# A statically ordered decoder layer: coarser places for background steps, a longer scan price, and pages waited for

## The chip, the cores and the metric

One Trainium2 chip, one of its cores. The metric is device microseconds of one execution of the program. Times of instructions come from one execution that the hardware profiler recorded; its microseconds are counted from the first recorded instruction.

## The reference

One decoder layer on x (1024 tokens, 1024 features), float32. `proj = rmsnorm(x) @ w_in` is cut into attention q, k, v (8 heads of 64), and q, k, v, output gate and input and forget gates of an mLSTM (4 heads of 128). The attention sums three dilated windows. The mLSTM goes by chunks: with `b` the running sum of the log forget gate and `m` a running maximum, it builds the scaled states and the heads' outputs. Both halves are normed and go through `w_out`; the result is added to x. Then follows a gated feed-forward part (`w_ffn_up` to 2 x 2816, a causal convolution of 3 taps, silu(gate) * value, `w_ffn_down`), added again, and a last norm.

## The kernel before, in words

**How precise matmuls are made.** A float32 product is made of three matmuls of a faster 4-byte type: every operand is split into a high and a low page, and `mm3` (the helper after `copy`) issues high x high, high x low, low x high. So matmuls come in threes.

**Stages.** The projections come first (`project`): 19 units, written out by hand in the string `order`. A unit "m" (mLSTM q or k of one head) or "h" (attention q and k of one head) makes two banks of 512 tokens, each from 8 threes of 512 columns, k = 0 to 7. A unit "g", "v" or "a" (gates, mLSTM values, attention values) makes 8 blocks of 128 tokens, each from 8 threes of 256 or 260 columns. The weights of unit n are named w*n* in the trace (w3 is the unit v0, w16 to w18 are the last three attention heads). Then `output` makes the product with `w_out`: first the mLSTM half (weights w0, w1 on the tiles ymh, yml), then, when all four attention groups are there, the attention half (w2, w3 on yh, yl). Its blocks are made by `o_block`, 4 threes of 512 columns each. Last come `upward` (tiles xb, W) and `downward` (A, B), which the change does not touch.

**What sets the order.** Every engine runs its instructions in the order in which the program was written, and waits in that order. The order is made when the program is built. The work is held in lanes: Python generators with a priority (a lower number goes first). A lane yields `need(...)`: the tiles it needs, free pages (`pg`, of 48 in SBUF, with `keep` more left over), free PSUM banks (`bk`). `Lanes.run` looks at the model's time on PE ("now"), computes for each lane the time at which its need is met (`when`), and takes the first lane by priority whose need has been met for 0.6 us (`SLACK`); if there is none, the one that is met first. The model (`Clock`) adds a price to an engine's time for each instruction; `Clock.cost` holds the prices. A `project` or `output` lane (priorities 10 and 11) always has something to run and so is what PE does when no other lane is ready: the **foreground**. All other lanes are **background**. A background step can come between two foreground matmuls only where the foreground yields.

Before the change an "m" or "h" unit yields after every three matmuls, a "g", "v" or "a" unit after every second three (`if k % 2`), and `o_block` after every three.

**The gate lane** (`gates`, priority 4). When the gates are projected, 16 transposes bring them into rows, DVE makes two scans over 1024 elements (`tensor_tensor_scan`: tiles gb and gm), then uu and four writes into the tile `rows`. PE transposes `rows` in 8 pieces of 68 x 68 and multiplies it 8 times with `sel` (8 columns each). The mLSTM lanes wait for what comes out. `Clock.cost` has no case for a scan: it falls to the last line for DVE, 0.095 + n * 0.0011 us.

**The attention lanes.** `stacks` (one per head, priority 3) takes the two projected banks, multiplies them by R into the page t, and splits t into the pages q1, q2 and kS with five copies and two subtractions on ACT and DVE. `scores` goes through heads and pairs of query blocks (matmuls bank<-kS,q), `soft` takes the exponent on ACT, `trans` transposes (bank<-ident,P), `evac_T` splits the result (tile PT), `values` multiplies (bank<-PT,av), `fold` and `att_norm` end a group of two heads, `att_t` and `y_trans` transpose it into yh, yl. At most three heads may lie ready in `heads` (`HL`) before `project` holds back the next. `stacks` takes its first page after `yield need(pg=4, keep=2, ...)` and the pages q1, q2, kS right after the second bank is evacuated, with no look at when those pages become free.

The output's attention half needs all of `yT["a", g]` and both its weights; the last of these (w3) is split only when `output` has taken w2.

Of the kernel before, what the change touches and what calls it, by code (L numbers as in the profile page):

```python
# [29 lines left out]
class Clock:  # L30
# [84 lines left out]
    def cost(self, eng, op, outs, ins, k):  # L115
        n = 1
        for d in (ins if op == "tensor_reduce" else outs)[0].shape[1:]:
            n *= d
        from_psum = any(a.tensor.name in self.psum for a in ins)
        if eng == "pe":  # L120
            dt = ins[0].dtype
            if dt == F32R:
                return n / 2246 + 0.004
            if dt == BF:
                return max(n, 64) / 2400 + 0.003
            return 0.11 if op == "transpose" else 2 * max(2 * n, 256) / 2300
        if eng == "act":
            c = (0.05 if from_psum else 0.1) + n * 0.000833 + 0.09 * (len(ins) + len(outs) - 2)
            for v in list(k.get("_a", ())) + list(k.values()):
                if isinstance(v, AF) and v in self.SETS:  # L130
                    if self.table not in (None, self.SETS[v]):
                        c += 1.3
                    self.table = self.SETS[v]
            return c
        if eng == "dve":
            if op == "reciprocal":
                return n * 0.0063
            fast = op in ("tensor_copy", "tensor_scalar", "memset") and not from_psum
            return 0.095 + n * (0.00058 if fast else 0.0011) + (0.06 if from_psum else 0) + (0.05 if len(ins) > 2 else 0) + 0.01 * (len(outs) - 1)
        if OP.pow in k.values():  # L140
            return 0.3 + n * 0.165
        return 0.1 + n * 0.00228
# [76 lines left out]
def need(*tiles, pg=0, bk=0, cond=None, keep=0, kb=0):  # L219

    return tiles, pg, bk, cond, keep, kb
# [3 lines left out]
def tile_hybrid_layer(ctx, tc, xT, x, w_t, w_v, w_g, w_o, w_uq, w_dq, params, fnw, c_id, c_att, c_sel,  # L225
# [23 lines left out]
    def page(name, dt=F32):  # L249
        slot[0] = freep.pop(0)  # L250
        t = pages.tile([128, PGW], dt, tag="pg", name=name)
        clk.floor[t.tensor.name] = slot[0]
        return t

    def free(*ts):
        for t in ts:
            freep.append(clk.last(t))
# [5 lines left out]
    def bank(name=None):  # L263
        t = min(freeb, key=clk.last)
        freeb.remove(t)
        return t
# [49 lines left out]
    def mm3(o, lh, ll, rh, rl, start, stop):  # L316
        pe.matmul(o, lh, rh, start=start, stop=False)
        pe.matmul(o, lh, rl, start=False, stop=False)
        pe.matmul(o, ll, rh, start=False, stop=stop)
# [64 lines left out]
    def wneed(whl, **k):  # L384
        return need(*[t for p in whl for t in p], **k)
# [8 lines left out]
    for o in order.split():  # L394
        n = int(o[1])
# [171 lines left out]
    def fin_ready(ps, hf):  # L567

        if hf < len(ps) and "R" in flags:
            return max(clk.ready(ps[hf]), 1e-9)  # L570
        return False

    def ml_conv(c, ps):

        h, isk = divmod(c, 2)
        for hf in range(2):
            yield need(pg=0 if hf else 2, cond=lambda: fin_ready(ps, hf))
            if hf == 0:
                z = page("mz")
                a = page("mqk")  # L580
            dve.tensor_mul(z[:, H[hf]], ps[hf], R[:, H[hf]])
            freebank(ps[hf])
        ch = 4 * isk + h
        cw = lambda j: pr[:, P_CW + ch * 4 + j:P_CW + ch * 4 + j + 1]
        yield need(z)
        act.activation(a[:, :S], z[:, :S], AF.Identity, scale=cw(3), bias=pr[:, P_CB + ch:P_CB + ch + 1])
        for j in (2, 1, 0):
            sh = 3 - j
            yield need(a)
            dve.scalar_tensor_tensor(a[:, sh:S], z[:, :S - sh], cw(j), a[:, sh:S], op0=OP.mult, op1=OP.add)  # L590
        free(z)
        yield need(a)
        act.activation(a[:, :S], a[:, :S], AF.Silu)
        qk[c] = a
# [42 lines left out]
    def project():  # L637

        for n, (kind, arg) in enumerate(plan):
            if n == len(plan) - 2:  # L640
                flags.add("late")
            if n == len(plan) - 1:
                flags.add("last")
            npg = {"mv": 2, "av": 4, "g": 4 if arg == 0 else 0}.get(kind, 0)
            yield need(pg=npg, cond=lambda: n in feed.done and (kind != "att" or len(heads) < HL))
            whl = feed.get(n)
            if kind in ("ml", "att"):
                (wh, wl), = whl
                ps = []
                for hf in range(2):  # L650
                    yield wneed(whl, bk=1, kb=FGB - 1 if "R" in flags else 1)
                    p = bank("fg")
                    if hf == 0:
                        lanes.add(ml_conv(arg, ps) if kind == "ml" else stacks(arg, ps), 3)
                    for k in range(8):
                        ks = slice(k * 128, (k + 1) * 128)
                        mm3(p, wh[:, ks], wl[:, ks], xh[k][:, H[hf]], xl[k][:, H[hf]], k == 0, k == 7)
                        if hf and n == len(plan) - 1:
                            free(xh[k], xl[k])
                        yield need()  # L660
                    ps.append(p)
            else:
                w = 260 if kind == "g" else 256
                if kind == "g" and arg == 0:
                    sg.extend(page(f"sg{i}") for i in range(4))
                if kind == "mv":
                    for h in (2 * arg, 2 * arg + 1):
                        t = page(f"va{h}")
                        vap.append(t)
                        va.append(t[:, :1032].rearrange("p (c j) -> p c j", j=129))  # L670
                        pool.memset(va[h][:, :, 128:129], 1.0)
                if kind == "av":
                    av[arg] = [page(f"av{arg}{i}", F32R) for i in range(4)]
                for i in range(8):
                    yield wneed(whl, bk=1, kb=FGB - 1)
                    p = bank("fg")
                    ts = slice(i * 128, (i + 1) * 128)
                    for k in range(8):
                        wh, wl = whl[k // 4]
                        ks = slice((k % 4) * w, (k % 4 + 1) * w)  # L680
                        mm3(p[:, :w], xh[k][:, ts], xl[k][:, ts], wh[:, ks], wl[:, ks], k == 0, k == 7)
                        if k % 2:
                            yield need()
                    lanes.add(evac_n(kind, arg, i, p, w), 3)
            feed.put(whl)
        flags.add("projected")

    def evac_n(kind, arg, i, p, w):
        yield need(p)
        {"g": evac_g, "mv": evac_mv, "av": evac_av}[kind](arg, i, p[:, :w])  # L690
        freebank(p)
        if i == 7:
            flags.add((kind, arg))
# [208 lines left out]
    def stacks(h, ps):  # L902
        for hf in range(2):
            yield need(pg=0 if hf else 4, keep=2, cond=lambda: fin_ready(ps, hf))
            if hf == 0:
                t = page("t")
            dve.tensor_mul(t[:, H[hf]], ps[hf], R[:, H[hf]])
            freebank(ps[hf])
        if h == 7:
            free(R)  # L910
        q1 = page("q1", F32R)
        q2 = page("q2", F32R)
        kS = page("kS", F32R)
        lo, up = slice(0, 64), slice(64, 128)
        A = slice(0, S)
        yield need(t)
        copy(q1[lo, A], t[lo, A])
        copy(kS[up, A], t[up, A])
        yield need(q1)
        dve.tensor_sub(q2[lo, A], t[lo, A], f32(q1[lo, A]))  # L920
        copy(q2[up, A], t[lo, A])
        yield need(kS)
        dve.tensor_sub(kS[lo, A], t[up, A], f32(kS[up, A]))
        yield need(q2)
        copy(q1[up, A], f32(q2[lo, A]))
        free(t)
        den = small.tile([128, 8], F32, name="aden", bufs=4)
        heads[h] = (q1, q2, kS, den)
# [184 lines left out]
    def o_block(p, hf, i, key, whl):  # L1113
        sl = slice(hf * 512, (hf + 1) * 512)
        ts = slice(i * 128, (i + 1) * 128)
        for k in range(4):
            yh, yl = yT[key, k]
            wh, wl = whl[k // 2]
            ws = slice((k % 2) * 512, (k % 2 + 1) * 512)
            mm3(p, yh[:, ts], yl[:, ts], wh[:, ws], wl[:, ws], k == 0, k == 3)  # L1120
            yield need()

    def add_h(i, hf, p):
        yield need(p, hp[i])
# [570 lines left out]
```

## Time and profile before

| | us |
|---|---|
| median of 3 runs | 1223.29 |
| lowest, highest | 1223.19, 1224.44 |
| the profiled execution's own time | 1226.69 |
| its span, first to last instruction | 1224.9 |

A row of the timeline gives the start, the time that the instruction (or a run of like ones) took, the engine, and what it wrote from what. Matmuls are pipelined, so the time that one took (0.39 us for 512 columns) is longer than its share of PE: what a matmul costs is the time from its start to the next one's start. PEld is the load of the stationary operand, which overlaps. "Idle before" in square brackets names what an engine waited for. The granted clock is a share of full speed: 1.00 is 2.4 GHz, 0.50 is 1.2 GHz, and a number in between is a mean over the stretch.

### The profile page before, as it was taken

What the parts mean: (1) busy time and instruction counts of PE and PEld (TensorE: products, weight loads), DVE (VectorE), ACT (ScalarE), POOL (GpSimd) and SP (SyncE); (2) the same over time, 40 slices, a digit from 0 to 9 for tenths busy, and PEclk for the clock granted to TensorE, in tenths of its full rate; (3) what the DMA queues carried; (4) which work ended last, traced back from release to release, by engine and by line L of the source; (5) the groups of instructions that cost most, each with busy time, mean ns of one, the idle gap of its engine ahead of it and who ended that gap; (6) DMA issues with size and microseconds to landing.
All of it is one profiled execution on the core that took longest, in us unless ns stands there. A gap on an engine that the chain in (4) does not pass through costs nothing.

```text
span 1224.9 us, 17354 instructions
## 1 busy us (share of the span) xinstructions
PE 1214.1 (99%) x6366; PEld 1028.9 (84%) x6366; DVE 889.7 (73%) x1642; ACT 589.5 (48%) x1139; POOL 255.3 (21%) x176
## 2 busy tenths in 40 slices
PE   9999999999999999999999999999999999999997
PEld 7899898988998888888888888888888888888886
DVE  6634573658886988645998787768777788988965
ACT  5464253437764675445763533434344353343553
POOL 0421032120212210211043413333332310000001
PEclk9999999999999999999999999999999999999999
DMA  9360917564256679243566663775633379423333
GB/s 364 151 225 18 206 70 275 114 162 165 94 125 167 225 254 245 69 146 142 121 221 179 207 232 113 205 242 132 194 115 126 127 299 410 135 86 97 94 102 139
DMA packets 64077, 208.01 MB, mean 170 GB/s; under 512 B 6644, under 2 KB 9972, under 8 KB 59000
## 3 DMA queue, kind: packets, MB, share of 16 engines
q1 hardware_dynamic: 57048, 135.80, 31.3%
q0 software_dynamic: 4352, 34.60, 14.0%
q10 hardware_dynamic: 2592, 36.50, 8.8%
q8 instruction: 50, 0.82, 0.3%
q14 instruction: 35, 0.29, 0.1%
HBM read 182.76 MB, written 93.32 MB: 225 GB/s over the span
## 4 chain that ended last, share of the span: by engine, by line
PE 96%; DVE 2%; DMA 1%; issue 0%; ACT 0%; POOLq 0%; POOL 0%; ACTq 0%; DVEq 0%
PE bank L153 96%; DMA h<-in_x_dram 1%; DVE P L153 0%; DMA w0r<-in_w_t_dram 0%; DVE rows L153 0%; DVE gb L153 0%; DVE gm L153 0%; DVE ams L153 0%; DVE uu L153 0%; DVE nmx L153 0%; ACT lf L153 0%; ACT sq L153 0%; DVE hq L153 0%; DVE h L153 0%; DVE OT L153 0%
## 5 line engine op out<-in xcount | busy, mean ns | idle before, releaser
L153 PE MATMUL bank<-xb,W 128*128 128x512 f32 x1848 | 428.9, 394 | 0.0
L153 PEld LDWEIGHTS bank<-xb,W 128*128 128x128 f32 x1848 | 346.9, 188 | 80.8
L153 PE MATMUL bank<-B,A 128*128 128x512 f32 x924 | 213.9, 393 | 0.0
L153 PEld LDWEIGHTS bank<-B,A 128*128 128x128 f32 x924 | 173.6, 188 | 40.1
L153 POOL TENSOR_TENSOR W<-ur,W 128x512 fp32r<-128x512 f32 x94 | 123.7, 1331 | 277.4 <-ACT W L153 134.5
L153 DVE SCALAR_TENSOR_TENSOR ua<-bank,pr,ua 128x512 f32<-128x512 f32 (+3 forms) x208 | 133.8, 646 | 25.1 <-ACT ua L153 19.0
L153 ACT ACTIVATE ua<-bank,pr 128x512 f32<-128x512 f32 (+1 forms) x84 | 64.9, 774 | 146.3 <-DVE bank L153 146.3
L153 DVE TENSOR_TENSOR bank<-bank,ut 128x512 f32<-128x512 f32 x84 | 58.2, 697 | 33.1 <-PE bank L153 31.7
L153 ACT ACTIVATE W<-ur 128x512 fp32r<-128x512 f32 x122 | 71.5, 622 | 16.1 <-DMA ur<-in_w_uq_dram 10.2
L153 ACT ACTIVATE A<-g 128x512 fp32r<-128x512 f32 x75 | 46.4, 626 | 60.0 <-DVE g L153 48.4
L153 POOL TENSOR_TENSOR rs<-st,half 128x1 f32<-128x1 f32 x16 | 11.2, 698 | 265.2 <-DVE st L153 265.2
L153 ACT ACTIVATE P<-P,nmx 128x128 f32<-128x128 f32 (+3 forms) x64 | 49.4, 773 | 25.0 <-DVE nmx L153 24.6
L153 DVE CUSTOM_DVE_ANT_0 P<-bank,matt 128x512 f32<-128x512 f32 (+3 forms) x96 | 50.6, 552 | 13.7 <-PE bank L153 13.5
L153 DVE TENSOR_TENSOR ut<-ut,bank 128x512 f32<-128x512 f32 x66 | 45.0, 682 | 19.7 <-PE bank L153 19.1
L153 DVE TENSOR_TENSOR A<-g,A 128x512 fp32r<-128x512 f32 x75 | 50.9, 685 | 7.0 <-ACT A L153 6.7
L153 DVE TENSOR_TENSOR hq<-hq,bank 128x512 f32<-128x512 f32 x56 | 36.6, 680 | 24.7 <-PE bank L153 24.7
L153 DVE TENSOR_TENSOR PT<-bank,PT 128x512 fp32r<-128x512 f32 (+1 forms) x80 | 47.8, 629 | 9.1 <-ACT PT L153 8.8
L153 ACT ACTIVATE B<-br 128x512 fp32r<-128x512 f32 x70 | 43.2, 621 | 22.7 <-PE bank L153 9.7
L153 DVE TENSOR_TENSOR B<-br,B 128x512 fp32r<-128x512 f32 x76 | 51.5, 683 | 3.3 <-ACT B L153 3.1
L153 DVE TENSOR_TENSOR W<-ur,W 128x512 fp32r<-128x512 f32 x60 | 43.9, 738 | 7.1 <-ACT W L153 6.5
L153 ACT ACTIVATE PT<-bank 128x512 fp32r<-128x512 f32 (+1 forms) x71 | 37.1, 551 | 23.6 <-PE bank L153 20.9
L153 PE MATMUL bank<-PT,av 128*128 128x256 f32 (+1 forms) x320 | 46.6, 279 | 0.0
(352 smaller groups left out, 2435.3 us busy)
## 6 DMA issues: line engine op xcount, KB each, us to landing
usum<-in_w_uq_dram POOLq DMA_DIRECT2D x4, 5632.0 KB, 34.1
ur<-usum SPq DMA_DIRECT2D x88, 256.0 KB, 4.1
ur<-in_w_uq_dram SPq DMA_DIRECT2D x66, 256.0 KB, 4.5
usum<-in_w_uq_dram ACTq DMA_DIRECT2D x2, 5632.0 KB, 20.7
usum<-usum ACTq DMA_DIRECT2D x2, 5632.0 KB, 21.8
tsum<-in_w_dq_dram POOLq DMA_DIRECT2D x4, 2816.0 KB, 19.0
gp<-ua SPq DMA_DIRECT2D x22, 512.0 KB, 3.0
g<-gp SPq DMA_DIRECT2D x22, 512.0 KB, 7.7
```

What stands on the lines that cost most here:

```text
L153: r = f(*a, **k)
```

## The change

A scan gets a price of its own in the model. "m" and "h" units yield after every second three matmuls, "g", "v" and "a" units after every fourth, `o_block` after every second. In `stacks` the lane yields once for t and three pages together, ahead of taking them. No instruction of the program is added or removed by the text of the diff; what changes is the order in which the lanes write them, and the pages and banks that they get.

```diff
--- before.py
+++ after.py
@@ -135,6 +135,8 @@
         if eng == "dve":
             if op == "reciprocal":
                 return n * 0.0063
+            if op == "tensor_tensor_scan":
+                return 0.05 + n * 0.0022
             fast = op in ("tensor_copy", "tensor_scalar", "memset") and not from_psum
             return 0.095 + n * (0.00058 if fast else 0.0011) + (0.06 if from_psum else 0) + (0.05 if len(ins) > 2 else 0) + 0.01 * (len(outs) - 1)
         if OP.pow in k.values():
@@ -657,7 +659,8 @@
                         mm3(p, wh[:, ks], wl[:, ks], xh[k][:, H[hf]], xl[k][:, H[hf]], k == 0, k == 7)
                         if hf and n == len(plan) - 1:
                             free(xh[k], xl[k])
-                        yield need()
+                        if k % 2:
+                            yield need()
                     ps.append(p)
             else:
                 w = 260 if kind == "g" else 256
@@ -679,7 +682,7 @@
                         wh, wl = whl[k // 4]
                         ks = slice((k % 4) * w, (k % 4 + 1) * w)
                         mm3(p[:, :w], xh[k][:, ts], xl[k][:, ts], wh[:, ks], wl[:, ks], k == 0, k == 7)
-                        if k % 2:
+                        if k % 4 == 3:
                             yield need()
                     lanes.add(evac_n(kind, arg, i, p, w), 3)
             feed.put(whl)
@@ -908,12 +911,12 @@
             freebank(ps[hf])
         if h == 7:
             free(R)
+        yield need(t, pg=3)
         q1 = page("q1", F32R)
         q2 = page("q2", F32R)
         kS = page("kS", F32R)
         lo, up = slice(0, 64), slice(64, 128)
         A = slice(0, S)
-        yield need(t)
         copy(q1[lo, A], t[lo, A])
         copy(kS[up, A], t[up, A])
         yield need(q1)
@@ -1118,7 +1121,8 @@
             wh, wl = whl[k // 2]
             ws = slice((k % 2) * 512, (k % 2 + 1) * 512)
             mm3(p, yh[:, ts], yl[:, ts], wh[:, ws], wl[:, ws], k == 0, k == 3)
-            yield need()
+            if k % 2:
+                yield need()
 
     def add_h(i, hf, p):
         yield need(p, hp[i])
```

## Rows read from the trace of the kernel before

**Rows 1.** The page: busy time, share of the span and instructions of each engine.

```profile
PE 1214.1 (99%) x6366; PEld 1028.9 (84%) x6366; DVE 889.7 (73%) x1642; ACT 589.5 (48%) x1139; POOL 255.3 (21%) x176
```

**Rows 2.** Engines by stretch: start:end, length, busy us (instructions) per engine, clock, DMA share, GB/s.

```profile
114.50:124.10 9.60, 8.61 (x48) 8.20 (x47) 3.53 (x7) 2.84 (x9) 3.62 (x2) 0.64 0.18 26
...
267.00:525.00 258.00, 256.66 (x1592) 227.81 (x1591) 203.20 (x488) 159.42 (x306) 54.08 (x26) 1.00 0.55 160
...
575.50:1004.60 429.10, 429.10 (x1859) 347.97 (x1858) 338.32 (x521) 190.25 (x336) 132.38 (x102) 1.00 0.57 178
```

**Rows 3.** Who made PE wait, whole span: us in total, times, longest.

```profile
PE bank L153 <- DVE lnk L153: 1.2, 1, 1.2
PE bank L153 <- DVE rows L153: 1.0, 2, 0.7
PE bank L153 <- DVE h L153: 0.8, 1, 0.8
PE bank L153 <- DVE w0h L153: 0.7, 1, 0.7
PE bank L153 <- ACT P L153: 0.4, 1, 0.4
```

**Rows 4.** DVE in order of time, 104 to 130: start us, us, instruction, count, idle before.

```profile
107.21 2.28 DVE L153 TENSOR_TENSOR_SCAN gb<-rst,lf 4x1024 f32<-4x1024 f32 x1 [3.56 <-ACT lf L153]
109.42 2.25 DVE L153 TENSOR_TENSOR_SCAN gm<-lf,li 4x1024 f32<-4x1024 f32 x1
111.78 1.21 DVE L153 TENSOR_TENSOR uu<-gb,gm 4x1024 f32<-4x1024 f32 x1
...
115.00 1.07 DVE L153 TENSOR_TENSOR rows<-uu,gm 4x896 f32<-4x896 f32 x1
116.00 1.21 DVE L153 TENSOR_TENSOR urow<-uu,urow 4x1024 fp32r<-4x1024 f32 x1
```

**Rows 5.** PE in order of time, 108 to 130.

```profile
114.49 0.28 PE L153 MATMUL bank<-w3l,xh 128*128 128x256 f32 x1
114.61 0.28 PE L153 MATMUL bank<-w3h,xl 128*128 128x256 f32 x1
115.22 0.25 PE L153 MATMUL bank<-ident,rows 68*128 68x68 f32 x1 [0.33 <-DVE rows L153]
116.12 0.66 PE L153 MATMUL bank<-ident,rows 68*128 68x68 f32 x7 [0.66 <-DVE rows L153]
116.71 1.46 PE L153 MATMUL bank<-rows,sel 4*128 4x8 f32 x8
118.11 0.58 PE L153 MATMUL bank<-w3h,xh 128*128 128x256 f32 x1
...
124.03 0.28 PE L153 MATMUL bank<-w3h,xh 128*128 128x256 f32 x1
124.15 0.28 PE L153 MATMUL bank<-w3l,xh 128*128 128x256 f32 x1
```

**Rows 6.** PE in order of time, 423 to 447, transposes between the matmuls of a projection.

```profile
427.15 0.49 PE L153 MATMUL bank<-ident,P 128*128 128x128 f32 x3
...
427.71 0.40 PE L153 MATMUL bank<-xl,w18h 128*128 128x512 f32 x1
...
428.87 0.93 PE L153 MATMUL bank<-ident,P 128*128 128x128 f32 x7
...
429.87 0.39 PE L153 MATMUL bank<-xl,w18h 128*128 128x512 f32 x1
...
434.26 0.39 PE L153 MATMUL bank<-xh,w18h 128*128 128x512 f32 x1
...
434.95 0.64 PE L153 MATMUL bank<-PT,av 128*128 128x256 f32 x4
```

**Rows 7.** PE in order of time, 490 to 512.

```profile
496.25 0.48 PE L153 MATMUL bank<-w0h,ymh 128*128 128x512 f32 x1
...
497.02 1.04 PE L153 MATMUL bank<-PT,av 128*128 128x256 f32 x8
```

**Rows 8.** PE in order of time, 510 to 530.

```profile
524.90 0.40 PE L153 MATMUL bank<-w2h,yh 128*128 128x512 f32 x1
```

**Rows 9.** POOL in order of time, 497 to 520.

```profile
519.87 2.41 POOL L153 TENSOR_TENSOR w3l<-wr,w3h 128x1024 fp32r<-128x1024 f32 x1 [8.53 <-ACT w3h L153]
```

**Rows 10.** DMA issues: out<-in, engine, count, KB each, median us from issue to landing.

```profile
wr<-in_w_t_dram SPq DMA_DIRECT2D x13, 512.0 KB, 8.8
```

**Rows 11.** ACT in order of time, 404 to 424, and PE, 423 to 447.

```profile
419.05 1.06 ACT L153 ACTIVATE q<-q 64x1024 fp32r<-64x1024 f32 x1
...
422.97 0.97 PE L153 MATMUL bank<-kS,q 128*128 128x128 f32 x6
```

## The prediction

> **What bounds the kernel now.** The page's busy shares come first: PE is busy 99% of the span, DVE 73%, ACT 48% [rows 1]. A busy PE need not be a fast one, so the windows by stage come next. From 575.5 to 1004.6 us PE starts 1859 matmuls, nearly all of 512 columns, in 429.10 us, 231 ns each: nothing is left between them. From 267 to 525 (attention) PE is idle 258.00 - 256.66 = 1.34 us. One stretch stands out: from 114.5 to 124.1 PE starts 48 matmuls in 9.6 us at a mean granted clock of 0.64 [rows 2]. The list of waits says the same: PE waited 4.1 us in all, 1.9 of it at the start (lnk, w0h), 1.0 for `rows`, 1.2 in attention (h, P) [rows 3]. So PE's own work sets the time. A new order that takes no matmul away can only return these waits and the clock that they cost, or add new ones.
>
> **The scan's price.** The model charged 0.095 + 1024 x 0.0011 = 1.22 us for a scan. The two scans and the next DVE step start at 107.21, 109.42 and 111.78, so one takes 2.2 to 2.4 [rows 4]. The new price is 0.05 + 1024 x 0.0022 = 2.30. So all that follows the scans is planned 2 x 1.08 = 2.16 us later. What was wrong is seen on PE: the last w3 matmul before the transposes starts at 114.61, and 0.12 later PE is free, but the first transpose starts at 115.22 and the second at 116.12 [rows 5], when DVE's write of `rows` at 115.00 + 1.07 = 116.07 is over [rows 4]. Seven transposes take 116.71 - 116.12 = 0.59, 0.08 each, so PE lost 115.22 - 114.73 = 0.49 and 0.90 - 0.08 = 0.82, in all **1.31 us**. A lane is taken at the first yield 0.6 us after its planned readiness, and yields there came every 6 x 0.12 = 0.72: the plan had `rows` ready between 113.4 and 114.1, where the chip had it at 116.07. With 2.16 more and yields every 1.44, PE comes to the transposes between 116.2 and 118.3: behind 116.07, so the wait goes. PE runs w3 matmuls meanwhile, of which enough are left: 27 from 118.11 to 124.03 alone [rows 5]. The mLSTM lanes behind `rows` start about 2 us later, under the next unit's matmuls.
>
> The clock is the larger part. After the waits and the narrow matmuls (8 of 68 columns, 8 of 8 columns), 27 w3 matmuls take 124.03 - 118.11 = 5.92 us, 0.22 each, where the same ones take 0.12 before and after [rows 5]: PE ran at 1.2 GHz instead of 2.4. That costs 5.92 - 27 x 0.12 = **2.7 us**, and the eight 8-column matmuls, 1.40 us together, may hold another 0 to 0.7 (at a narrow transpose's 0.08 each they would take 0.7). Without the waits the light stretch is 0.6 + 1.4 = 2.0 us instead of 118.11 - 114.73 = 3.4. No row shows whether the clock falls after that. The ends are "falls as before" (0 gained) and "stays" (2.7 to 3.4 gained). Nearest is attention, where PE waits of 0.8 and 0.4 us [rows 3] lie among narrow matmuls and the clock stays at 1.00 [rows 2]. I take "stays".
>
> The Trainium skill, "TensorE: Matmul & The Clock Gate", Part 4, says that PE transposes do not count as PE being busy for the clock. By that rule the stretch would still look idle and the time would be rival 1's; attention's 1.00, with its many transposes, speaks against it only weakly, because wide matmuls stand among them.
>
> **Yields after every six.** First, does a change from foreground to background cost PE anything? Three transposes and the matmul behind them take 427.71 - 427.15 = 0.56, seven and the matmul 429.87 - 428.87 = 1.00 [rows 6]. Four more transposes cost 0.44, 0.11 each; 0.56 - 3 x 0.11 = 0.23 is left for the matmul, and three plain ones take 434.95 - 434.26 = 0.69, 0.23 each [rows 6]. A switch costs nothing, so fewer switches gain **0**.
>
> What coarser yields cost is delay. A background step that is ready waits until a six ends, at most one more three, 0.69 us. From 423 to 500 the foreground runs in 22 stretches between background steps; 14 hold an odd number of threes (one at 434.26 [rows 6], the last but one at 496.25 [rows 7]) and would end 0.69 later: up to 14 x 0.69 = 9.7 us if all lie on one chain, 0 if other background work fills in. What hides it is foreground: the attention half starts at 524.90 [rows 8] and its last input, w3l, is ready at 519.87 + 2.41 = 522.28 [rows 9]. The **cover is 2.6 us**; beyond it PE waits. I take 0, because DVE, 203 of 258 us busy there [rows 2], paces the heads as much as PE's places do, and because what background loses foreground gains: the last heads' projections end earlier. Both ends, 0 and 9.7 - 2.6 = 7.1, are kept. The 1.2 us of waits in attention may go or come back elsewhere: I take 0 and keep -1.2.
>
> Work that is moved with the lanes: weight loads on SP (512 KB, 8.8 us to land) [rows 10] and their splits on POOL (2.41 us each) [rows 9] go out up to 0.69 us later, against a unit of 48 x 0.23 = 11 us that they run ahead. Nothing else on SP, ACT's or POOL's queues changes in number.
>
> **Pages in `stacks`.** The lane now waits for t and three pages before it takes them. Behind it wait five copies and two subtractions on ACT and DVE, then `scores`. Where cover is small, the last write of q ends at 419.05 + 1.06 = 420.11 and the head's scores start at 422.97 [rows 11]: 2.9 us. Pages that come later than that would add to attention's delay above, earlier ones change nothing: 0, with the same 2.6 us behind it. A gain is bounded by attention's 1.2 us of PE waits, which are counted already.
>
> **The sum.** Against the profiled execution's own 1226.69 us (span 1224.9 and 1.8 around it): 1226.69 - 1.31 - 2.7 = 1222.7. The median of the runs is 1223.29, 3.40 lower. I cannot see whether the timed runs have the fall of the clock. The gap is about its price (2.7 to 3.4), which would fit runs that mostly lack it; then only 1.31 is to be had. I count half of 2.7: 1223.29 - 1.31 - 1.35 = **1220.6**.
>
> **Rivals.** (1) **The clock falls anyway**, after 2.0 us of narrow matmuls. For it: the fall came in just this stretch. Against: 1.31 us of plain idling is gone. Time 1223.29 - 1.31 = 1222.0. Chance 0.18.
>
> (2) **Attention ends too late**: slower. Place: between the last head's scores and 524.90. For it: 14 of 22 stretches get longer, and the cover is 2.6. Against: DVE's share, earlier projections. At a delay d PE waits d - 2.6: at 9.7 the time is 1220.6 + 7.1 = 1227.7; it is slower than before by over 0.2% (2.45 us, about what a measurement here tells from no change) from d = 2.6 + 2.7 + 2.45 = 7.7 on, or from 5.0 if that wait lowers the clock too, at 2.7. Chance 0.27.
>
> (3) **The change does not do what it says**: the order is made anew as a whole, another step before `rows` (the chain has four more DVE writes) is planned too early, and PE waits as before: 1223.3, give or take attention's 1.2. Chance 0.08.
>
> **How the numbers follow.** The forecast has 0.47; its own range is 1223.29 - 1.31 - 3.4 = 1218.6 to 1222.0. It is faster by over 0.2% if at least 2.45 - 1.31 = 1.14 of the clock's 2.7 us is in the timed runs, or part of it and attention's 1.2: four in five of 0.47, 0.38; with rival 2 below d = 2.8 (0.05) and rival 3's luck (0.01), faster 0.44. Same: 0.09 of the forecast, 0.18, 0.05 of rival 3, and 0.06 of rival 2, 0.38. Slower: 0.16 of rival 2 and 0.02 of rival 3, 0.18. The range goes from 1223.29 - 1.31 - 3.4 - 1.2 = 1217.4 to rival 2's 1227.7; beyond it lies attention's delay with a fall of the clock on top.
>
> **What would show it.** Right: the row of PE's waits for `rows` is gone, the transposes of `rows` start after DVE's last write, the granted clock is 1.00 from 114 to 125, the w3 matmuls keep 0.12, and the stretches of foreground between background steps are all multiples of six without a wait of PE before w2h,yh. Rival 1: no wait but a clock under 1.00 there. Rival 2: a wait of PE, or w3l within a few tenths of the first w2h,yh. Wrong altogether: gains or losses behind 575, where I expect PE at 231 ns a matmul as now.

## The result and the profile after

The changed kernel takes 1230.38 us (median of 4 runs, 1230.10 to 1230.62); the kernel before took 1223.72 beside it. The ratio is 1.0053, 95% interval 1.0041 to 1.0065: **slower by half a per cent**, 6.7 us, where 1220.6 was forecast and the range ended at 1227.7. The profiled execution's own time is 1230.62, its span 1228.8 us. All medians here and below are of executions in the chip's fast state; one of the six of kernel e9 below (1319.21 us at a granted clock of 0.85) is left out.

The page's busy shares, as [rows 1]:

```profile
PE 1214.0 (99%) x6366; PEld 1027.6 (84%) x6366; DVE 893.0 (73%) x1649; ACT 583.1 (47%) x1131; POOL 251.2 (20%) x175
```

PE is as busy as before, and the other shares move by at most one point: a page of shares does not show the loss. The windows by stretch do, as [rows 2] (start:end, length, busy us and instructions of PE, PEld, DVE, ACT and POOL, granted clock, DMA share, GB/s):

```profile
114.50:123.00 8.50, 8.50 (x76) 8.41 (x75) 3.81 (x7) 4.06 (x11) 3.56 (x2) 1.00 0.00 0
...
310.00:318.00 8.00, 2.64 (x10) 1.62 (x9) 3.95 (x9) 0.41 (x1) 0.00 (x0) 0.92 0.41 168
318.00:335.00 17.00, 16.33 (x112) 15.77 (x113) 13.49 (x36) 12.12 (x24) 2.48 (x2) 0.84 0.01 1
335.00:525.00 190.00, 189.18 (x1193) 168.55 (x1192) 148.43 (x359) 114.62 (x224) 35.74 (x18) 1.00 0.62 175
...
575.50:1008.50 433.00, 433.00 (x1884) 351.25 (x1884) 340.99 (x526) 192.06 (x344) 132.02 (x102) 1.00 0.57 177
```

The gate stretch (114.5 to 123) is whole now: 76 matmuls in 8.5 us at clock 1.00, where 48 took 9.6 us at 0.64 [rows 2]. The up projection runs at 433.0 / 1884 = 0.230 us a matmul, as before. The loss is new and stands in one place: from 310 to 318 PE works 2.64 of 8.00 us, and the clock is 0.92 and then 0.84 up to 335. Who made PE wait, as [rows 3]:

```profile
PE bank L155 <- DVE nmx L155: 5.2, 2, 4.8
PE bank L155 <- DVE PT L155: 1.7, 2, 1.2
PE bank L155 <- DVE lnk L155: 1.2, 1, 1.2
PE bank L155 <- DVE w0h L155: 0.3, 1, 0.3
```

The 1.0 us for `rows` is gone, so are h and P; nmx and PT have come, 6.9 us together.

**The gates.** DVE in order of time, as [rows 4], and PE, as [rows 5]:

```profile
109.59 2.25 DVE L155 TENSOR_TENSOR_SCAN gm<-lf,li 4x1024 f32<-4x1024 f32 x1
111.94 1.22 DVE L155 TENSOR_TENSOR uu<-gb,gm 4x1024 f32<-4x1024 f32 x1
...
115.18 1.07 DVE L155 TENSOR_TENSOR rows<-uu,gm 4x896 f32<-4x896 f32 x1
```

```profile
117.73 0.66 PE L155 MATMUL bank<-ident,rows 68*128 68x68 f32 x8
118.33 1.05 PE L155 MATMUL bank<-rows,sel 4*128 4x8 f32 x8
```

DVE's last write of `rows` ends at 115.18 + 1.07 = 116.25; PE now comes to the transposes at 117.73, inside the forecast 116.2 to 118.3, and does not wait.

**The new wait.** PE, then DVE, around 311 us:

```profile
311.67 0.39 PE L155 MATMUL bank<-xh,w13l 128*128 128x512 f32 x1
316.88 0.58 PE L155 MATMUL bank<-PT,av 128*128 128x256 f32 x1 [4.82 <-DVE nmx L155]
318.67 0.91 PE L155 MATMUL bank<-PT,av 128*128 128x256 f32 x3 [1.21 <-DVE PT L155]
```

```profile
300.05 2.60 DVE L155 TENSOR_TENSOR q<-t,q 64x1024 fp32r<-64x1024 f32 x1 [0.49 <-ACT q L155]
313.96 1.16 DVE L155 CAST PT<-bank 128x384 fp32r<-128x384 f32 x2 [11.31 <-DMA parked<-yh]
315.14 1.22 DVE L155 TENSOR_TENSOR kS<-t,kS 64x1024 fp32r<-64x1024 f32 x1
316.39 0.42 DVE L155 CUSTOM_DVE_ANT_0 P<-bank,matt 128x256 f32<-128x256 f32 x1
```

PE ends the projection of attention head 3 (w13), finds a value product next in its order and waits 4.82 us for DVE's step on a block of scores (its last part is nmx). DVE has sat since 302.65 in front of one cast, 11.31 us, and what it waits for is not an engine but a DMA: the store `parked<-yh`. The page that this PT tile takes was a page of yh. The lane frees it as soon as the store of the mLSTM output is issued, and the store still reads it. The queues say why it reads so long. SP's queue, after and before:

```profile
294.42 0.33 SPq L895 DMA_DIRECT2D parked<-yh  x1
296.06 0.33 SPq L895 DMA_DIRECT2D parked<-yl  x1
```

```profile
280.49 0.33 SPq L892 DMA_DIRECT2D parked<-yh  x1
281.99 0.33 SPq L892 DMA_DIRECT2D parked<-yl  x1
```

DMA issues near it, after and before (out<-in, queue, count, KB each, median us to landing; a landing behind the window's end is not given):

```profile
usum<-usum ACTq DMA_DIRECT2D x1, 5632.0 KB, 22.1
...
parked<-yl SPq DMA_DIRECT2D x1, 512.0 KB, 19.0
```

```profile
usum<-usum ACTq DMA_DIRECT2D x1, 5632.0 KB, 21.4
parked<-yh SPq DMA_DIRECT2D x1, 512.0 KB, 2.6
parked<-yl SPq DMA_DIRECT2D x1, 512.0 KB, 3.4
```

Before, the stores went out at 280.49 and 281.99 and landed in 2.6 and 3.4 us; ACT's queue issued one of the background sums (5632 KB, usum to usum) 14 us later:

```profile
295.79 0.48 ACTq L789 DMA_DIRECT2D usum<-usum  x1
```

After, the stores go out at 294.42 and 296.06, 14 us later than before, while that sum, issued at 291.33, is under way:

```profile
291.33 0.48 ACTq L792 DMA_DIRECT2D usum<-usum  x1
```

A store of 512 KB now takes 19.0 us to land. The program's order is fixed, so whatever needs DVE's results waits with it.

### The profile page after: what moved, and what is told of

Its sections match the earlier page's. It is cut to its first block, busy times and chain, and to the rows that moved or that the text cites. A ratio compares the mean times of both kernels' runs of the same rounds, so it can differ in the third digit from the quotient of the medians.

```text
span 1228.8 us, 17335 instructions
## 1 busy us (share of the span) xinstructions
PE 1214.0 (99%) x6366; PEld 1027.6 (84%) x6366; DVE 893.0 (73%) x1649; ACT 583.1 (47%) x1131; POOL 251.2 (20%) x175
## 4 chain that ended last, share of the span: by engine, by line
PE 95%; DVE 2%; DMA 2%; issue 0%; ACT 0%; POOLq 0%; POOL 0%; ACTq 0%; SPq 0%; DVEq 0%
PE bank L155 95%; DMA wr<-in_w_t_dram 1%; DVE P L155 1%; DMA w0r<-in_w_t_dram 0%; DVE PT L155 0%; DVE nmx L155 0%; DVE ams L155 0%; DVE yl L155 0%; DVE h L155 0%; DVE kS L155 0%; DVE ya L155 0%; ACT sq L155 0%; DVE hq L155 0%; DVE t L155 0%; DVE OT L155 0%
## 5 line engine op out<-in xcount | busy, mean ns | idle before, releaser
L155 PEld LDWEIGHTS bank<-PT,av 128*128 128x128 f32 x320 | 44.6, 193 | 9.6 <-DVE nmx L155 5.3
```

What stands on the lines that cost most here:

```text
L155: r = f(*a, **k)
```

## Experiments

Theory: a page that a store still reads, and the store is slow because of the sum (A). Rivals: the coarser yields themselves make attention late (B); the store is slow by its place in its queue, not by the sum (A'); the store's slowness holds up what queues behind it, whatever the page (D). Theory E, in experiment 6, is on why the store came late. Every kernel ran beside the kernel before, whose runs span 1222.3 to 1226.7 with medians of 1224.3 to 1224.4.

### 1. One DMA moved

```diff
-        for to, src, add in order:
-            yield need(cond=lambda: clk.eng.get("pe", 0.0) > t)
+        for n, (to, src, add) in enumerate(order):
+            yield need(cond=lambda: clk.eng.get("pe", 0.0) > t + (30 if (n, dt) == (4, 55) else 0))
```

> The changed kernel with one DMA moved: the fifth of the eight background sums (usum to usum, 5632 KB, issued on ACT's queue at 291 us) is issued about 30 us later. The order of all other instructions stays. Theory A (a page that a store still reads): the changed kernel's loss is one wait of DVE, 11.3 us, for the store parked<-yh, which reads the page that a PT tile takes over; the store is slow because the sum's transfer shares the DMA engines with it. Expected: DVE's wait for parked under 3 us, PE's wait of 4.8 us behind the last w13 matmul gone or under 1, clock 1.00 from 310 to 335, time 1221 to 1224. Theory B (coarser places): the delay of the background steps makes attention late whatever DVE waits for, so PE's idle time of about 7 us only moves; time 1227 to 1231. Theory A' (the store is late by its place in its queue, not by the sum): the store still lands near 313, nothing changes, 1230.

Measured: 1221.34 us, ratio 0.9977 (0.9967 to 0.9986). The sum went out at 321.2 instead of 291.3. The store, issued at 294.76 as late as in the changed kernel, lands fast again:

```profile
parked<-yh SPq DMA_DIRECT2D x1, 512.0 KB, 2.6
```

DVE in order of time, and who made PE wait:

```profile
300.40 2.60 DVE L155 TENSOR_TENSOR q<-t,q 64x1024 fp32r<-64x1024 f32 x1 [0.50 <-ACT q L155]
304.64 1.15 DVE L155 CAST PT<-bank 128x384 fp32r<-128x384 f32 x2 [1.64 <-PE bank L155]
```

```profile
PE bank L155 <- DVE lnk L155: 1.2, 1, 1.2
PE bank L155 <- DVE PT L155: 0.5, 1, 0.5
PE bank L155 <- DVE nmx L155: 0.3, 1, 0.3
```

The same cast now follows 1.64 us after the instruction before it, and waits for PE, not for a DMA. PE's long wait is gone. All engines run the same instructions in the same order as in the changed kernel but for this one issue, so the collision's price is 1230.38 - 1221.34 = **9.0 us** (8.7 between the own times of the profiled executions, 1230.62 and 1221.92). An estimate from the rows of the changed kernel comes to the same: PE's two waits, 4.82 + 1.21 us, and the clock, 17.00 x (1 - 0.84) = 2.7 us from 318 to 335, are 8.7. Theory A holds; A' falls with the 2.6 us, and B falls as the explanation of the loss. What is left of the change is a gain of 0.23%, 2.8 to 3.1 us.

### 2 to 4. The parts

The coarser yields without the pages' wait were not run. The other parts:

```diff
 e2: the changed kernel with the yields of before
 e3: the changed kernel without
-            if op == "tensor_tensor_scan":
-                return 0.05 + n * 0.0022
 e4: the kernel before with these two lines
```

> The changed kernel with the old yields (after every three of 512 columns, every six of 256), so the scan's price and the pages' wait alone. Theory B: the loss is gone, 1219 to 1222.5. Theory A: the order is made anew, so whether a critical page is taken from under a store is open: without such a wait of DVE or ACT over 3 us 1220 to 1222.5, with one up to 1230; the time goes with that wait, not with the yields. Both: PE's wait for rows is gone, worth 1.3 us against the kernel before, 4 in a profile where the clock fell.

> The changed kernel with the old price of a scan, so the coarser yields and the pages' wait alone. Theory B: as slow as the changed kernel or slower by the 1.3 us of the wait for rows, 1229 to 1233. Theory A: PE's wait for rows comes back (1.3 us); beside it the loss is there only if again an engine on the chain waits for a store: 1223 to 1225 without, 1230 to 1233 with it.

> The kernel before with the scan's price alone. Both theories: PE's wait for rows goes. If the fall of the clock behind it is in the timed runs, 1219 to 1220; if it is in the profiled execution alone, 1222 to 1223 (1.3 us less than before). A new wait for a store or a page elsewhere would show as a wait of DVE or ACT of several us and take the time above 1224.

| kernel | scan price | yields | pages' wait | us | ratio to before (95%) |
|---|---|---|---|---|---|
| changed | new | coarse | yes | 1230.38 | 1.0053 (1.0041, 1.0065) |
| e2 | new | old | yes | 1220.16 | 0.9966 (0.9953, 0.9978) |
| e3 | old | coarse | yes | 1231.83 | 1.0064 (1.0049, 1.0079) |
| e4 | new | old | no | 1221.65 | 0.9979 (0.9970, 0.9989) |

e2 has no wait of DVE or ACT for a store (its stores go out at 276.3 and 277.8, the sum at 292.0) and is the quickest so far: 4.2 us ahead of the kernel before. e3 waits again (DVE 11.1 us for the store, PE 1.0 for `rows`): 1.45 us above the changed kernel. e4, the scan's price alone, gains 1224.41 - 1221.65 = 2.76 us (by its interval 1.3 to 3.7), between the two outcomes that were expected. The pages' wait beside it gains another 1.5 (e4 to e2). So of three edits two gain and one costs: 10.2 us from e2 to the changed kernel, 9.0 of them by way of the collision. The 1.2 us that are left (e2 to e1) are not explained.

### 5. The page held back

```diff
             nc.sync.dma_start(parked[2 * h + j], f32(hl[j][:, :S]))
+        t0 = clk.eng["pe"]
+        yield need(cond=lambda: clk.eng["pe"] > t0 + 22)
+        for t in hl:
+            nc.gpsimd.memset(f32(t[:, 1024:1032]), 0.0)
         free(*hl)
```

> The changed kernel, but the two pages of each parked store are given back only 22 us of planned PE time after the store is issued (with a small write by POOL that ends their use). The store still goes out beside the sum. Theory A (page taken from under a store): the store again lands some 17 to 20 us after its issue, but no engine waits for it for more than 3 us; PE's wait near 311 is gone; 1220 to 1223. Rival D (the slow store itself holds up the transfers behind it, the weight load for w15 above all): the page does not matter, PE still waits several us between 310 and 335, 1226 to 1231.

Measured: 1225.87 us, ratio 1.0010 (1.0001, 1.0019). The store is as slow as in the changed kernel:

```profile
usum<-usum ACTq DMA_DIRECT2D x1, 5632.0 KB, 21.5
...
parked<-yl SPq DMA_DIRECT2D x1, 512.0 KB, 18.4
```

But no engine waits for it any more, and PE is busy 25.00 of 25.00 us from 310 to 335. So the slow store alone makes nothing wait there; store and page together do. D falls as the cause of the wait at 311. The time missed the expected 1220 to 1223, though: PE waits at another place, from 461.5 to 463.6 us, for nmx. All its waits of that kind (us in total, times, longest):

```profile
PE bank L155 <- DVE nmx L155: 2.5, 3, 2.1
```

That wait is at a place in attention that the change of pages re-planned; which step was planned too early there was not traced further. It does not hold all of the 4.5 us by which e5 lies above e1: the profiled execution, 1224.34 us, is the fastest of ten, at a mean granted clock of 0.999, and the other nine, 1225.7 to 1226.7, were granted 0.996 to 0.998. Where the clock fell in those, and what the rest is, stays open.

### 6. Why the store came late

In the changed kernel the mLSTM head's output sg is ready at 277.6 us and PE transposes it, the step ahead of the store, only at 289.36. In the kernel before, sg was ready at 272.00 + 2.19 = 274.19 and the transposes came at 276.71, 2.5 us behind. So of the 13.9 us by which the store moved, 3.4 are sg itself, 9.2 the longer pause behind it (11.8 instead of 2.5), and 1.3 the steps from there to the store. DVE and PE of the changed kernel:

```profile
275.42 2.18 DVE L155 SCALAR_TENSOR_TENSOR sg<-nm,msq,sg 128x128 f32<-128x128 f32 x8
```

```profile
289.36 0.60 PE L155 MATMUL bank<-ident,sg 128*128 128x128 f32 x4
```

The lane asks there for six free pages (`pg=2, keep=4`). The experiment asks for five:

```diff
-        yield need(pg=2, keep=4, cond=...)
+        yield need(pg=2, keep=3 if key[0] == "m" else 4, cond=...)
```

> The changed kernel, but the mLSTM heads' last transposes ask for five free pages (two to take, three to keep) instead of six. Theory E (the store came late because its lane waited for pages, not because places on PE are fewer): in the changed kernel sg is ready at 277.6 us and its transposes start at 289.4; here they start within 5 us of sg, the store goes out before the sum at about 291 and lands in under 5 us; no long wait of DVE, 1220 to 1223. Theory B' (fewer places on PE delay the store step by step): the transposes still start after 285, the store collides again, 1229 to 1231.

DVE and PE of this kernel:

```profile
275.03 2.18 DVE L155 SCALAR_TENSOR_TENSOR sg<-nm,msq,sg 128x128 f32<-128x128 f32 x8
```

```profile
279.91 0.60 PE L155 MATMUL bank<-ident,sg 128*128 128x128 f32 x4
```

Now 279.91 - 277.21 = 2.7 us lie between them instead of 11.8; the stores go out at 285.1 and 287.4, before the sum (291.5), and land in 2.6 and 2.9 us. So the long pause ahead of the store was the lane's wait for pages that other lanes held, not a lack of places on PE (E holds for the pause). The time again missed what was expected: 1226.24, ratio 1.0012 (1.0003, 1.0021). The wait at 311 is gone, but PE waits 1.9 us for OT near 437 and 0.9 for PT, in an order that is new from 280 on. Which lane held the pages was not tried.

### 7 to 11. Which yields

The kernel of e2 (new price, pages' wait) or of e1, with the yields changed at one place each:

```diff
 e7: e2 with o_block after every six
 e8: e1 with o_block after every three, as before
 e9: e2 with the 256-column units after every three, the finest
 e10: e2 with the 512-column units after every six
 e11: e2 with the 256-column units after every twelve
```

> Scan price and pages' wait, old yields in the projections, coarse yields in the output product alone. If the coarse yields cost something of their own there (later attention tail, later norm steps), it shows against the same kernel with old yields everywhere (1220.2): theory B'' 1221 to 1222; if they are free, 1219.8 to 1220.6, with w3l still ready before the first w2h,yh.

> The changed kernel with the fifth sum 30 us later (1221.3) and old yields in the output product, so coarse yields in the projections alone, without the collision. If the 1.2 us that it is above the kernel with old yields everywhere come from the output product's yields, 1219.8 to 1220.6; if from the projections', 1221 to 1222, the same as with both.

> The other direction: scan price and pages' wait, with yields after every three matmuls in all projections (the 256-column units too, which before yielded after every six) and in the output product. If a switch between foreground and background cost PE anything, some tens of switches more would show as a longer time with no wait: 1221 to 1223. If a switch is free, PE's time outside waits is the same, and the time is 1219 to 1221 with attention's waits of PE no longer than with the old yields (0.6 us).

> Scan price and pages' wait, coarse yields in the 512-column projections alone (every six), old ones elsewhere. The units in which mLSTM heads 2 and 3 and attention heads 0 to 2 run beside the projections are mostly of this kind. If these yields bring the late store, it goes out behind the sum at about 291 us and some engine waits for it or not by the page's luck (1220 to 1231); if not, the store goes out before 285 as with the old yields and the time is 1220 to 1222.

> Scan price and pages' wait, coarse yields in the 256-column projections alone (every twelve of 256 columns), old ones elsewhere. If these yields bring the late store, it goes out behind the sum at about 291 us (1220 to 1231); if not, before 285, 1220 to 1222.

| kernel | changes from foreground to background and back | us | ratio (95%) |
|---|---|---|---|
| e9, finest | 281 | 1219.84 | 0.9966 (0.9953, 0.9978) |
| e2, old yields | 275 | 1220.16 | 0.9966 (0.9953, 0.9978) |
| e7, coarse in o_block | 271 | 1220.23 | 0.9966 (0.9952, 0.9980) |
| e11, coarse in 256-column units | 265 | 1222.64 | 0.9987 (0.9977, 0.9996) |
| e8, coarse in both projections, sum moved | 261 | 1222.97 | 0.9991 (0.9982, 1.0000) |
| e10, coarse in 512-column units | 249 | 1232.59 | 1.0072 (1.0057, 1.0087) |

The counts are taken from PE's order of matmuls. More changes do not cost: e9 with the most is level with e2, and e7's yields in o_block are free. e11 missed its 1220 to 1222: it is 2.5 us slower than e2, with PE's waits alike (2.3 us in total against 2.2), and why is not known. e10 alone brings the collision back, at the same place, and at 1232.59 lies past its expected 1231; DVE and PE's waits there:

```profile
313.19 1.16 DVE L155 CAST PT<-bank 128x384 fp32r<-128x384 f32 x2 [10.88 <-DMA parked<-yh]
```

```profile
PE bank L155 <- DVE nmx L155: 5.3, 2, 4.4
PE bank L155 <- DVE PT L155: 2.5, 2, 1.3
```

So it is the 512-column units' yields that move the store (it goes out at 294.1 there, at 281.9 in e11). e8 does not bear out that o_block's yields hold the 1.2 us between e1 and e2: it is slower, not quicker, than e1, by a new wait of PE for PT, 1.9 us. Its windows show what such a wait does beyond itself:

```profile
460.00:468.00 8.00, 8.00 (x53) 7.07 (x52) 7.76 (x28) 5.97 (x15) 4.15 (x3) 1.00 0.10 17
468.00:476.00 8.00, 6.14 (x40) 5.94 (x39) 6.64 (x17) 4.21 (x11) 0.00 (x0) 0.79 1.00 199
476.00:484.00 8.00, 8.00 (x52) 7.18 (x51) 5.51 (x18) 5.29 (x12) 0.00 (x0) 1.00 1.02 244
```

From 468 to 476 PE works 6.14 of 8.00 us and the granted clock is 0.79: after the wait, which ends at 470.56, it is 0.50 from 472 to 474, which is 1.2 GHz. The profiled execution's own time was 1224.2; the 11 runs lie in two bunches, seven from 1222.5 to 1223.1 at a mean granted clock of 0.998 to 0.999 and four from 1224.2 to 1224.7 at 0.997 to 0.998. So the same kernel loses more clock in some executions than in others; that it is at this wait in all four is not shown, as only one of them was profiled.

## Why the prediction was wrong, and where it was right

**The scan's price: right.** PE comes to `rows` behind its last write, the wait is gone, and PE runs 1.00 through the stretch. The forecast took "the clock stays" and half of 2.7 us as its worth in the timed runs, 1.31 + 1.35 = 2.66 with the wait; e4, this edit alone, gained 2.76. That the two are so close is luck in part: the half was a mean between two ends, and the interval of e4's gain is 1.3 to 3.7. That the timed runs have the fall of the clock in part is borne out by their granted clocks: of the 20 runs of the kernel before beside e4, the seven quickest (1222.3 to 1223.6) were granted 0.999 to 1.000 on the mean and the other 13 (1223.9 to 1225.9) 0.997 to 0.998; e4's ten, 1221.1 to 1222.1, all 0.998 to 0.999. Rival 1 is out: 16 narrow matmuls in 1.65 us (117.73 to 118.33 + 1.05), 8 of them transposes, leave the clock at 1.00. By the rule of the Trainium skill that was set against the trace there ("TensorE: Matmul & The Clock Gate", Part 4: transposes do not count as PE being busy) the prediction had rival 1's time, and that did not come; these eight transposes do not show whether the rule itself holds.

**A switch costs nothing: right,** as far as ten changes can show it: e9, e2 and e7 are level (1219.84 to 1220.23) with 281, 275 and 271 changes.

**What coarser yields cost: wrong, and here the forecast failed.** The step reads "A background step that is ready waits until a six ends, at most one more three, 0.69 us", and, for the moved work, "weight loads on SP and their splits on POOL go out up to 0.69 us later" and "Nothing else on SP, ACT's or POOL's queues changes in number". Three things were missed. First, a lane that is late can find its pages gone, and then it waits for pages, not for PE: the store moved by 14 us, not by 0.69, and 9.2 of them are that pause (e6). Second, the list of what is moved left out the mLSTM's stores on SP; moved 14 us, they crossed the sum on ACT's queue, and a landing of 2.6 to 3.4 us became 19 (e1). Third, the cover was looked for at one place only, in front of the output's attention half; the page of the store had a cover of its own. For these two stores the kernel before shows no wait, because there they went out some 14 us before the sum. For an earlier pair it does: issued at 184.31 and 185.10, behind a sum of 5632 KB issued at 183.61, they took 21.7 and 22.2 us to land, and POOL waited for one of their pages. From the kernel before, who waited for the parked stores (us, times), and their landings:

```profile
  POOL w9l L153: 7.5, 1
DMA to landing us min/median/max: 2.6/6.2/22.2
```

PE was busy throughout that wait (9.00 of 9.00 us from 198 to 207; POOL went on at 206.18), so there the same collision cost PE nothing. What the change did was to put it on DVE, ahead of a step that PE needed; the trace of before could have warned of it. The planner did not see it either: the parked stores are issued without an entry in its model, so their pages count as free at once. The general warning, that DMAs issued from several queues share the same 16 engines and interleave, stands in the Trainium skill ("Trainium Kernel Development and Optimization", Key Constraints); this trace agrees, with 2.6 us alone and 19.0 beside 5632 KB.

**Rival 2** had the sign and the mechanism's kind (background too late, a PE wait, the clock on top) but not the place. At its own place the change came close: w3l is ready at 523.52 + 4.79 = 528.31 and the first w2h,yh starts at 528.57, so the cover went from 2.6 us [rows 8, 9] to 0.3 and held. POOL and PE after:

```profile
523.52 4.79 POOL L155 TENSOR_TENSOR w3l<-wr,w3h 128x1024 fp32r<-128x1024 f32 x2 [6.89 <-ACT w3h L155]
```

```profile
528.57 0.39 PE L155 MATMUL bank<-w2h,yh 128*128 128x512 f32 x1
```

**Pages in `stacks`: mis-sized.** Taken at 0; beside the new scan price it gained 1.5 us (e4 to e2). Waits in attention hold 0.7 of it: e4 still has PE's waits of h and P (1.3 us) and e2 has 0.6 us of nmx and PT in their place. The rest is not traced. The bound kept for it was 1.2.

**The sum.** All but the collision: 1221.34 - 1224.4 = -3.1 us measured in e1, against -2.7 forecast from before's 1223.29. The collision, +9.0, was not in the sum, and the range's upper end of 7.1 us for attention did not hold it.

## What to carry to other kernels

Where a planner writes the order, an edit of where it may switch is an edit of every transfer's time: list the stores and large copies on each queue with their issue times before and after, and look for two that can change places. A page under a store is not free when the store is issued; price its landing at the slow end (19 to 22 us here), not the fast one. When PE is at 99%, the gain left is in single waits and in the clock that falls after them, and the versions that keep the scan's price, the pages' wait and the finer yields in the projections (e2, e7, e9, all near 1220) are quicker than both kernels.

## What the runs showed that was not expected

One kernel loses the clock in some executions and not in others. e8, with a wait of PE of 1.9 us, lies in two bunches some 1.7 us apart, and e6, with one of the same length, in 1224.5 to 1224.7 at a granted clock of 0.999 (three runs) and 1226.1 to 1226.7 at 0.997 to 0.998 (seven). The kernel before has such a place too, the gate stretch, and its profiled execution, 1226.69 us, lay 2.3 to 3.4 us above its medians, while the changed kernel's lay 0.2 above: its four runs, with the longer wait of 4.82 us, were all granted 0.995 to 0.996.
